# Output projection's first two weight tiles cast inside the planned attention stage, last rows returned by ScalarE, one conditioning vector computed in the recurrent mixer

## The chip, the cores and the metric

The kernel runs on one core of a Trainium2 chip. The core has five engines that work at the same time, each in order through its own queue: TensorE (PE, matrix products into PSUM banks; its weight loads are listed apart as PEld), VectorE (DVE), ScalarE (ACT), GpSimd (POOL) and SyncE (SP, which here only issues DMA transfers). The metric is the device time of one execution in microseconds; lower is better. A few runs are made, and their median is the time given.

## The reference

One sequence of 512 tokens with 1024 channels goes through two layers. Layer 0 mixes tokens by a gated linear recurrence (HGRN2, 8 heads, chunks of 32 tokens); layer 1 by attention in three groups of 8 heads with dilations 1, 4 and 16. Each is followed by a SwiGLU feed-forward block, and each block is modulated by vectors computed from one conditioning vector `c`. Cut to what the change touches:

```python
h = x
for layer in range(DEPTH):                       # 2
    mod = (cond @ ada_w[layer] + ada_b[layer])[:, None, :]
    sh1, sc1, g1, sh2, sc2, g2 = jnp.split(mod, 6, axis=-1)
    u = rms_norm(h, norm_g[layer, 0]) * (1.0 + sc1) + sh1
    y = hgrn2_mixer(...) if layer == 0 else dilated_attention_mixer(u, cos, sin, attn_w_in[0], attn_w_out[0])
    h = h + (1.0 + g1) * rms_norm(y, norm_g[layer, 1])
    u = rms_norm(h, norm_g[layer, 2]) * (1.0 + sc2) + sh2
    h = h + (1.0 + g2) * rms_norm(swiglu_ffn(u, ffn_w_in[layer], ffn_w_out[layer]), norm_g[layer, 3])

def dilated_attention_mixer(u, cos, sin, w_in, w_out):
    # per group: q, k with rope on the first 32 of 128 channels of a head, softmax over a window,
    # then the three groups' outputs weighted by softmax of their log sums
    o = jnp.einsum('gbsh,gbshd->bshd', wts, jnp.stack(outs, axis=0))
    return o.reshape(B, S, D_MODEL) @ w_out
```

All inputs are float32. In what follows, vector (l, v) is the v-th of the six vectors of layer l in the order of the split: (0, 5) is layer 0's last gate `g2`, (1, 4) is layer 1's second scale `sc2`.

## The kernel before

**Products.** A float32 product is made of three products of rounded parts: an operand is split into `hi` (a cast by ScalarE) and `lo` (the rest, a subtraction by VectorE), and `three` (L573) issues hi·hi, hi·lo and lo·hi; hence the three lines L574, L575 and L576 wherever weights are multiplied. `cut` and `split` do the same for activations: `oh` and `ol` are the parts of the attention's output `oT`.

**Weights.** `items` (L505 on) is one list of everything that SyncE loads during the kernel, in order: weight tiles of 1 MB (128 x 2048 numbers), and between them the tiles of `ada_w`, from which the modulation vectors are computed. `weave(ws, others, first, every)` strews the entries of `others` between weight tiles, one for each `every` tiles. Class `Stream` walks the list: a loaded tile occupies one of two `raw` buffers, and the next load is issued when a buffer is released; hi and lo parts occupy one of three places. `process_to` casts a weight tile as a whole (L89, L90), `pieces` in pieces (L109, L110), and runs the work of an `ada` entry where it stands in the list.

**A modulation vector.** A vector (1024 numbers) comes from four `ada` tiles (`ada_item`: two halves of the vector, each from two tiles). A tile gives four multiply-adds of 128 x 512 on VectorE (L390, L392); after two tiles GpSimd sums over the partitions (L394). A scale or shift then becomes a column form by four `to_col` operations per half (L404); a gate is finished by `row_fin` with a 512 KB pair of rows.

**The attention stage** (about 675 to 1105 us) has an order of its own. Class `Plan` takes every operation of the stage as a task with a cost, what it reads and writes, and in some cases a goal time; each task gets a due time from the tasks behind it, and the planner simulates the engines and lays down one order per engine. `next_weights` hands the next raw tile of the list to the plan, `plan.place` a buffer (`"hl"` is one of the three hi/lo places). `sevens` is a unit of one head and one of the groups 1 and 2; it leaves q and k of 128 x 512 in `qk`, of which the first 32 partitions carry the rotary embedding. Those 32 rows are copied to `rows` (an own 128 x 256 tile named `shared`), rotated by VectorE in `turned` (L2015) and brought back: for group 0 by ScalarE, for groups 1 and 2 by DMA on SyncE's queue (L2027), four of 32 KB for a unit.

**The stage's end.** The loop at L2425 runs `condition` up to `heads_end`, the index in `items` behind the last head's tiles; the plan then is laid down (L2428), and the items from `heads_end` on, the four tiles of `attn_w_out`, are taken by `mixer_out` (L684), whose order is written by hand. It multiplies the attention's output with `attn_w_out`: eight slices `kt` of the contraction (one head each), four token blocks in four PSUM banks `y0` for the first 512 columns, then `y1` for the others. Its first tile is taken at kt 0, its second at kt 4, each with a whole cast right there. Between these products the table `tail` puts what is left of the last two heads: `pv_n(6)` and the scores of head 7's group 2 behind kt 0 (L1897, L1812), `merge_r(7)` (L1833 to L1849) behind kt 2, `merge_n(7)` behind kt 3, the transposes `flips_r(7)` (L1861) behind kt 4. ScalarE and VectorE work in the order in which these lines stand.

Of the kernel before, what the change touches and what calls it, by code (L numbers as in the profile page):

```python
# [10 lines left out]
F32 = mybir.dt.float32  # L11
# [12 lines left out]
NH = 8  # L24
# [233 lines left out]
class Place:  # L258
# [8 lines left out]
    @property  # L267
    def t(self):
        return self.box[0]
# [22 lines left out]
def block_kernel(tc, x, c, positions, ada_w, ada_b, norm_g, hgrn_w_in, lower, hgrn_norm_g, hgrn_w_out,  # L292
                 attn_w_in, attn_w_out, ffn_w_in, ffn_w_out, inv_freq, out):
    nc = tc.nc
    act, dve, pool, pe = nc.scalar, nc.vector, nc.gpsimd, nc.tensor
    x2, out2 = x[0], out[0]
    V4 = lambda t: t.rearrange("p (a b) -> p a b", a=4)
    L4 = lambda a: a.rearrange("p (l r) -> p r l", r=4)
    R4 = lambda a: a.rearrange("p (r l) -> p l r", r=4)

    with ExitStack() as ctx:
# [29 lines left out]
        h = base.tile([P, NT, D], F32, name="h")  # L331
# [119 lines left out]
        def ada_seq(*vecs):  # L451

            res, last = [], None
            for l, v in vecs:
                for hf in range(2):
                    res.append([ada_item(l, v, hf, 0)])
                    res.append(([fin_item(*last)] if last else []) + [ada_item(l, v, hf, 1)])
                    last = (l, v, hf)
            return res + [[], [fin_item(*last)]]
# [15 lines left out]
        def weave(ws, others, first, every=1):  # L475

            res, o, n = [], list(others), 0
            for i, w in enumerate(ws):
                res.append(w)
                while i >= first + n * every and o:  # L480
                    res += o.pop(0)
                    n += 1
            return res + [i for g in o for i in g]

        items = []
        W = hgrn_w_in[0]
        hg = []
# [5 lines left out]
        hg_o = [wtok(hgrn_w_out[0], kq, hf * 512) for hf in range(2) for kq in range(2)]  # L493
# [10 lines left out]
            return a, [wrow(ffn_w_out[l], j) for j in range(NF // 2)]  # L504

        gate_loads, gate_fins = ada_halves(0, 5)
        items += weave(hg, ada_seq((0, 2), (0, 4), (0, 3)), 1) + gate_loads[0]
        items += weave(hg_o, gate_loads[1:2], 0)
        f0a, f0b = ffn_ws(0)
        n0 = 2 * PLAIN[0]  # L510
        items += weave(f0a[:n0], gate_loads[2:] + [[fin] for fin in gate_fins], 2) + f0a[n0:]
        items += weave(f0b, ada_seq((1, 1), (1, 0), (1, 4)), 0, 0.69)
        AW = attn_w_in[0]

        def av(g, hf):
# [2 lines left out]
        by_seven = lambda g: g > 0  # L518
# [5 lines left out]
        order, at = [], []  # L524
# [28 lines left out]
        for hd in range(5, NH):  # L553
            pairs(hd)
        woven(late[6:], 2)
        heads_end = len(items)
        items += [wtok(attn_w_out[0], kq, hf * 512) for hf in range(2) for kq in range(2)]
        f1a, f1b = ffn_ws(1)
        items += f1a + weave(f1b[:9], ada_seq((1, 5)), 0) + f1b[9:]
        st = Stream(nc, wp, items, 2, 3)  # L560
# [1078 lines left out]
        for p in range(4):  # L1639
# [11 lines left out]
            for k in range(2):  # L1651
# [5 lines left out]
                if k == 1:  # L1657
                    for i in range(2):
                        n = fl.n + i
                        g = {}  # L1660
# [257 lines left out]
        def ACT(cost, fn, r=(), w=(), **k):  # L1918
            plan.add("ACT", cost, lambda e: fn(), r, w, **k)

        def DVE(cost, fn, r=(), w=(), **k):
            plan.add("DVE", cost, lambda e: fn(), r, w, **k)
# [25 lines left out]
        def done_with_raw():  # L1948
            load_next()
# [40 lines left out]
        def next_weights():  # L1990
            while True:
                item = st.items[at_item[0]]
                at_item[0] += 1
                if item[0] in ("w", "quarters", "half"):
                    return queue.pop(0)
                condition(item)
# [15 lines left out]
        t_of = lambda i: [[a[:, i, k] for a in (th, tl)] for k in range(4)]  # L2012
        t1, T3, T4, t2 = (t_of(i) for i in range(4))

        def turned(g, rows, q, k):  # L2015


            rot = slot("rot", 1, [P, 256], mk)
            DVE(0.37, lambda: dve.stream_shuffle(rot.t, rows.t, [(i + 16) % 32 for i in range(32)]), [rows(i) for i in range(4)], [rot()])
            DVE(0.36, lambda: dve.tensor_mul(rot.t, rot.t, cs[:, 1]), w=[rot()])  # L2020
            DVE(0.36, lambda: dve.tensor_mul(rows.t, rows.t, cs[:, 0]), w=[rows(i) for i in range(4)])
            DVE(0.36, lambda: dve.tensor_add(rows.t, rows.t, rot.t), [rot()], [rows(i) for i in range(4)])
            if g:
                for i, t in enumerate((q, k)):
                    for n in range(2):
                        o = (2 * i + n) * 32
                        COPY(lambda t=t, n=n, o=o: nc.sync.dma_start(t.t[0:32, n * 256:n * 256 + 256], rows.t[o:o + 32]),  # L2027
                             [rows(2 * i + n)], [t(n)])
                return
            for i, t in enumerate((q, k)):  # L2030
                for hf in range(2):
                    def back_to(i=i, t=t, hf=hf):
                        dst, src = t.t[0:32], rows.t[i * 64 + hf * 32:i * 64 + hf * 32 + 32]
                        act.copy(L4(dst)[:, 2 * hf:2 * hf + 2], src.rearrange("p (r l) -> p r l", r=2))
                    ACT(0.62, back_to, [rows(2 * i + hf)], [t(0), t(1)])

        def new_rows():
            def make():
# [5 lines left out]
        def sevens(g, hd):  # L2044
# [53 lines left out]
            def products_2():  # L2098
                first, both, u2, u4 = s_["b"]
                xs = s_["xs"]  # L2100
                rows = new_rows()
                q, k = (slot("qk", 6, [P, S], mk) for _ in range(2))
                heads[hd]["q", g], heads[hd]["k", g] = q, k

                def queries(b, n):
                    sl = (lo, hi)[n]
                    ACT(0.38, lambda: act.activation(rows.t[n * 32:n * 32 + 32], b.t[0:32, lo], AF.Copy, scale=-SCALE), [b()], [rows(n)])
                    ACT(0.36, lambda: act.activation(q.t[:, sl], b.t[:, lo], AF.Copy, scale=-SCALE), [b()], [q(n)])

                def keys(n, src, b):  # L2110
                    sl = (lo, hi)[n]
                    DVE(0.36, lambda: dve.tensor_add(k.t[:, sl], xs.t[:, (lo, hi)[src]], b.t[:, lo]), [xs(src), b()], [k(n)])
                    ACT(0.38, lambda: act.copy(rows.t[64 + n * 32:96 + n * 32], k.t[0:32, sl]), [k(n)], [rows(2 + n)])
                run(first, 1, 3, a_of(1, 0), False)
                queries(first, 0)
                run(u4, 1, 0, t1, False)
                ACT(0.36, lambda: act.copy(xs.t[:, hi], u4.t[:, lo]), [u4()], [xs(1)], urgent=True)
                run(u2, 1, 2, T4, False)
                keys(1, 1, both)
                keys(0, 0, u2)  # L2120
                run(u4, 1, 1, a_of(1, 1), False)
                queries(u4, 1)
                turned(g, rows, q, k)
            return [(prepare_1, products_1), (prepare_2, products_2)]

        def plain(g, hd):
# [275 lines left out]
            ticks.add(n + 11, lambda: [flipped(i, "p0", "PN", range(1, 4), 0), flipped(i, "pn", "PN", range(4), 1)])  # L2402
            ticks.add(n + 12, lambda: sums_n(i))

        steps = []
        for kind, g, i in order:
            if kind == "v":
                steps += [("v", None, None, k, *p) for k, p in enumerate(value_unit(g - 1, i))]
# [4 lines left out]
        for n, (kind, g, hd, k, prepare, go) in enumerate(steps):  # L2413
# [8 lines left out]
            go()  # L2422
            if kind == "qk" and by_seven(g):
                ticks.tick()
        while at_item[0] < heads_end:  # L2425
            condition(st.items[at_item[0]])
            at_item[0] += 1
        with tc.manual_schedule(engines=ORDERED | {mybir.EngineType.SP}):  # L2428
            planned = plan.run()
        st.done, st.taken = heads_end, st.taken + sum(k == "qk" and not by_seven(g) for k, g, _ in order)  # L2430
        for st_ in heads.values():
            for name, p in st_.items():
                if isinstance(p, Place):
# [41 lines left out]
```

## Time and profile before

| | us |
| --- | --- |
| median of three runs | 1515.64 |
| lowest and highest | 1515.46, 1519.24 |
| the profiled execution | 1515.5 |
| its span | 1513.8 |
| TensorE busy in the span | 1480.4 (98%) |
| VectorE, ScalarE, GpSimd busy | 1115.9, 792.1, 197.2 |
| mean granted TensorE clock | 0.994 |

Loads that the change moves, from issue to landing in the median: 1 MB of `ada_w` 5.0 us, 1 MB of `ffn_w_out` 4.8 us. Tables of stretches give the busy microseconds of each engine per 25 us; a timeline gives start and duration of an instruction and, in brackets, how long its engine was idle before it and what ended that. Line numbers are those of the kernel before.

### The profile page before, as it was taken

To read this page: it belongs to the slowest core of one execution; us is meant where nothing else is said; L and a number is where in the kernel's file an instruction comes from. 1 tells how busy PE (TensorE), PEld (TensorE's weight loads), DVE (VectorE), ACT (ScalarE), POOL (GpSimd) and SP (SyncE) were. 2 spreads that over 40 slices of the span, in tenths; PEclk is the share of its full clock that TensorE was granted. 3 is DMA by queue.
4 is the path that set the end of the run, shared out by engine and by line. 5 is a ranking of instruction groups with operands and counts; after the bars stand their busy time and mean duration, and the time that the engine had idled before them with its cause. 6 is when DMAs were issued, how large, how long until landed. Compare 5 with 4: busy or idle time off the path is not lost. (4 is left out here: it accounts for less than half of the span.)

```text
span 1513.8 us, 25130 instructions
## 1 busy us (share of the span) xinstructions
PE 1480.4 (98%) x9807; PEld 1324.4 (87%) x9807; DVE 1115.9 (74%) x1904; ACT 792.1 (52%) x1462; POOL 197.2 (13%) x174
## 2 busy tenths in 40 slices
PE   8999999999999999999999999999979999999998
PEld 6777888898999988778999998999968899999886
DVE  4577767487788787777898888887656968887633
ACT  4433443363555532366648787378745545555231
POOL 1011211031111102140001101010002211110100
PEclk9999999999999999999999999999989999999999
DMA  9654444125333356623254442543323333334531
GB/s 303 181 172 132 160 140 167 56 84 167 112 111 106 115 179 235 236 99 125 88 151 140 133 133 88 164 122 94 92 74 126 92 104 112 111 109 143 198 109 56
DMA packets 210535, 201.35 MB, mean 133 GB/s; under 512 B 8376, under 2 KB 168304, under 8 KB 210160
## 3 DMA queue, kind: packets, MB, share of 16 engines
q1 hardware_dynamic: 207440, 192.97, 40.5%
q10 hardware_dynamic: 1952, 6.65, 1.2%
q8 instruction: 77, 1.26, 0.3%
q0 software_dynamic: 1024, 0.13, 0.2%
q14 instruction: 42, 0.34, 0.1%
HBM read 192.31 MB, written 5.31 MB: 131 GB/s over the span
## 5 line engine op out<-in xcount | busy, mean ns | idle before, releaser
L89 ACT CAST hi<-raw 128x2048 fp32r<-128x2048 f32 x45 | 85.9, 1909 | 144.4 <-DMA raw<-in_ffn_w_out_dram 71.4
L90 DVE TENSOR_TENSOR lo<-raw,hi 128x2048 fp32r<-128x2048 f32 x45 | 107.5, 2392 | 55.4 <-ACT hi L89 55.3
L574 PE MATMUL ps_mm<-uh,hi 128*128 128x512 f32 (+1 forms) x400 | 146.3, 366 | 0.0
L575 PE MATMUL ps_mm<-ul,hi 128*128 128x512 f32 (+1 forms) x400 | 144.3, 361 | 1.0 <-DVE ul L674 1.0
L576 PE MATMUL ps_mm<-uh,lo 128*128 128x512 f32 (+1 forms) x400 | 144.6, 361 | 0.0
L2007 PE MATMUL ps_mm<-apart,hiq 128*128 128x256 f32 (+1 forms) x608 | 142.4, 327 | 0.0
L2007 PEld LDWEIGHTS ps_mm<-apart,hiq 128*128 128x128 f32 x608 | 99.9, 188 | 8.1
L574 PE MATMUL ps_mm<-hi,oh 128*128 128x512 f32 x240 | 95.2, 397 | 6.7 <-ACT hi L89 6.7
L575 PE MATMUL ps_mm<-lo,oh 128*128 128x512 f32 x240 | 95.1, 396 | 3.6 <-DVE lo L90 3.5
L2007 PE MATMUL ps_mm<-apart,loq 128*128 128x256 f32 (+1 forms) x304 | 97.8, 322 | 0.1
L989 PE MATMUL ps_mm<-th,hiq 128*128 128x256 f32 x340 | 93.9, 276 | 0.0
L989 PE MATMUL ps_mm<-tl,hiq 128*128 128x256 f32 x340 | 93.9, 276 | 0.0
L989 PE MATMUL ps_mm<-th,loq 128*128 128x256 f32 x340 | 93.9, 276 | 0.0
L980 DVE TENSOR_TENSOR loq<-raw,hiq 128x1024 fp32r<-128x1024 f32 x68 | 80.2, 1222 | 18.4 <-ACT hiq L976 18.4
L574 PEld LDWEIGHTS ps_mm<-uh,hi 128*128 128x128 f32 x400 | 75.5, 189 | 19.8 <-issue 8.4
L575 PEld LDWEIGHTS ps_mm<-ul,hi 128*128 128x128 f32 x400 | 75.6, 189 | 12.1 <-DVE ul L674 1.4
L576 PEld LDWEIGHTS ps_mm<-uh,lo 128*128 128x128 f32 x400 | 75.5, 189 | 11.4
L960 POOL TENSOR_TENSOR raw<-raw 128x512 f32<-128x512 f32 x34 | 45.0, 1324 | 305.2 <-DVE spare L956 146.5
L976 ACT CAST hiq<-raw 128x1024 fp32r<-128x1024 f32 x68 | 68.0, 1047 | 17.4 <-DVE raw L964 16.5
L2007 PE MATMUL ps_mm<-uh,hiq 128*128 128x256 f32 x256 | 72.5, 283 | 4.0 <-ACT ps_mm L2092 3.0
L2007 PE MATMUL ps_mm<-uh,loq 128*128 128x256 f32 x256 | 71.6, 280 | 0.2 <-DVE loq L2050 0.2
L2007 PE MATMUL ps_mm<-ul,hiq 128*128 128x256 f32 x256 | 71.5, 279 | 0.0
(502 smaller groups left out, 4619.0 us busy)
## 6 DMA issues: line engine op xcount, KB each, us to landing
raw<-in_ada_w_dram SPq DMA_DIRECT2D x40, 1024.0 KB, 5.0
raw<-in_ffn_w_in_dram SPq DMA_DIRECT2D x136, 256.0 KB, 3.4
raw<-in_ffn_w_out_dram SPq DMA_DIRECT2D x22, 1024.0 KB, 4.8
raw<-in_attn_w_in_dram SPq DMA_DIRECT2D x64, 256.0 KB, 4.3
raw<-in_hgrn_w_in_dram SPq DMA_DIRECT2D x12, 1024.0 KB, 5.3
raw<-in_attn_w_in_dram SPq DMA_DIRECT2D x12, 1024.0 KB, 5.0
raw<-in_ffn_w_in_dram SPq DMA_DIRECT2D x10, 1024.0 KB, 5.6
raw<-in_attn_w_in_dram SPq DMA_DIRECT2D x16, 512.0 KB, 5.2
```

Of the source, the lines that this page charges most:

```text
L89: self.nc.scalar.copy(hi, t)
L90: self.nc.vector.tensor_sub(lo, t, hi.bitcast(F32))
L574: pe.matmul(ps, ah, bh, start=start, stop=False, skip_group_check=part)
L575: pe.matmul(ps, ah, bl, start=False, stop=False, skip_group_check=part)
L576: pe.matmul(ps, al, bh, start=False, stop=stop, skip_group_check=part)
L960: pool.tensor_add(r[:, 2], r[:, 2], r[:, 0])
L976: act.copy(hi, src)
L980: dve.tensor_sub(lo, src, hi.bitcast(F32))
L989: pe.matmul(ps, w[x][:, a], us[kt][y], start=begin and kt + m == 0, stop=kt == 3 and m == 2, skip_group_check=True)
L2007: pe.matmul(dst(), x, y, start=begin and i == 0, stop=i == len(todo) - 1, skip_group_check=True)
```

## The change

Three things are edited.

1. **Conditioning.** Vector (1, 4) leaves layer 0's `ffn_w_out` stage (`f0b`) and goes between the four tiles of the recurrent mixer's output projection (`hg_o`), two entries for a tile. Gate (0, 5) stood at the end of the mixer's weights and in `ffn_w_in`'s first tiles; its first two tiles are now in the latter, its last two and its second finish in `f0b`, where `weave` puts an entry for every 0.8 tiles instead of 0.69.
2. **Output projection.** `heads_end` goes. The first two `attn_w_out` tiles are taken by `next_weights` inside the plan and cast there in halves of 128 x 1024 by ScalarE and VectorE, with the plan's end as goal; `mixer_out` finds them in `st.ready`.
3. **Rows.** In the units of groups 1 and 2 of the last head (`hd == NH - 1`) the rotated rows go back by four ScalarE copies of 32 x 256 each, instead of four DMAs.

```diff
         gate_loads, gate_fins = ada_halves(0, 5)
-        items += weave(hg, ada_seq((0, 2), (0, 4), (0, 3)), 1) + gate_loads[0]
-        items += weave(hg_o, gate_loads[1:2], 0)
+        items += weave(hg, ada_seq((0, 2), (0, 4), (0, 3)), 1)
+        items += weave(hg_o, [g for g in ada_seq((1, 4)) if g], 0, 0.5)
         f0a, f0b = ffn_ws(0)
         n0 = 2 * PLAIN[0]
-        items += weave(f0a[:n0], gate_loads[2:] + [[fin] for fin in gate_fins], 2) + f0a[n0:]
-        items += weave(f0b, ada_seq((1, 1), (1, 0), (1, 4)), 0, 0.69)
+        items += weave(f0a[:n0], gate_loads[:2] + [gate_fins[:1]], 2) + f0a[n0:]
+        gate = gate_loads[2:]
+        rest = ada_seq((1, 1), (1, 0))
+        items += weave(f0b, gate + [gate_fins[1:] + rest[0]] + rest[1:], 0, 0.8)
...
-        heads_end = len(items)
         items += [wtok(attn_w_out[0], kq, hf * 512) for hf in range(2) for kq in range(2)]
...
-        def turned(g, rows, q, k):
+        def turned(g, rows, q, k, last=False):
...
-            if g:
+            if g and not last:
                 for i, t in enumerate((q, k)):
                     for n in range(2):
...
                     def back_to(i=i, t=t, hf=hf):
                         dst, src = t.t[0:32], rows.t[i * 64 + hf * 32:i * 64 + hf * 32 + 32]
-                        act.copy(L4(dst)[:, 2 * hf:2 * hf + 2], src.rearrange("p (r l) -> p r l", r=2))
-                    ACT(0.62, back_to, [rows(2 * i + hf)], [t(0), t(1)])
+                        if g:
+                            act.copy(dst[:, hf * 256:hf * 256 + 256], src)
+                        else:
+                            act.copy(L4(dst)[:, 2 * hf:2 * hf + 2], src.rearrange("p (r l) -> p r l", r=2))
+                    ACT(0.38 if g else 0.62, back_to, [rows(2 * i + hf)], [t(hf)] if g else [t(0), t(1)])
...
-                turned(g, rows, q, k)
+                turned(g, rows, q, k, hd == NH - 1)
...
-        while at_item[0] < heads_end:
-            condition(st.items[at_item[0]])
-            at_item[0] += 1
+        for _ in range(2):
+            raw, p = next_weights(), plan.place("hl", 3, lambda: st.part_tiles(0))
+            for n in range(2):
+                two = slice(n * 1024, n * 1024 + 1024)
+                ACT(1.0, lambda raw=raw, p=p, two=two: act.copy(p.t[0][:, two], raw.t[:, two]), [raw()], [p("h", n)], goal=clock[0])
+                DVE(1.15, lambda raw=raw, p=p, two=two: dve.tensor_sub(p.t[1][:, two], raw.t[:, two], p.t[0][:, two].bitcast(F32)),
+                    [raw(), p("h", n)], [p("l", n)], goal=clock[0])
+            done_with_raw()
+            after.append(p)
         with tc.manual_schedule(engines=ORDERED | {mybir.EngineType.SP}):
             planned = plan.run()
-        st.done, st.taken = heads_end, st.taken + sum(k == "qk" and not by_seven(g) for k, g, _ in order)
+        st.ready += [tuple(p.t) for p in after]
+        st.done, st.taken = at_item[0], st.taken + sum(k == "qk" and not by_seven(g) for k, g, _ in order)
```

Since a planner lays down the attention's order, the diff does not show where ScalarE's instructions land. Its rows at the end of the stage before, where `oh` are the parts of the attention's output, `hi` the whole cast of the first `attn_w_out` tile, `ps_a` the banks of transposes, L2107 and L2108 the copies of q out of its product bank into the 32 rows (`shared`) and into `qk`, L2280 the exponentials:

```order
L2113 COPY shared<-qk_10725 32x256 x2
L2280 ACTIVATE h,sN_10528<-h,nN_10183 128x256 x2
L570 CAST oh_11055<-oT_6093 128x512
L570 CAST oh_11056<-oT_6094 128x512
L570 CAST oh_11057<-oT_6095 128x512
L89 CAST hi_11074<-raw_10695 128x2048
L2359 COPY h<-ps_a_10955 128x384
L2107 ACTIVATE shared<-ps_mm_10885 32x256
L2280 ACTIVATE h,sN_10528<-h,nN_10183 128x256
L2280 ACTIVATE h,sN_10528<-h,nN_10183 128x128
L2375 COPY oT_late_6099<-ps_b_10686 128x4x128
L2359 COPY h<-ps_a_10962 128x512
```

The same place now. L2433 are the half casts (`hiq_10842` of the first tile, `hiq_10930` of the second), L2036 the returned rows of group 1:

```order
L2036 COPY qk_10628<-shared 32x256 x2
L2036 COPY qk_10629<-shared 32x256 x2
L2433 CAST hiq_10842<-raw_10695 128x1024
L2433 CAST hiq_10930<-raw_10962 128x1024
L571 CAST oh_11071<-oT_6093 128x512
L571 CAST oh_11072<-oT_6094 128x512
L571 CAST oh_11073<-oT_6095 128x512
L2363 COPY h<-ps_a_10959 128x384
L2433 CAST hiq_10930<-raw_10962 128x1024
L2111 ACTIVATE shared<-ps_mm_10817 32x256
L2117 COPY shared<-qk_10725 32x256 x2
L2111 ACTIVATE shared<-ps_mm_10887 32x256
```

and the rows that follow, where L2112 copies q from its two product banks and L2036 returns the rows of group 2:

```order
L2284 ACTIVATE h,sN_10528<-h,nN_10183 128x256 x3
L2284 ACTIVATE h,sN_10528<-h,nN_10183 128x128
L2379 COPY oT_late_6099<-ps_b_10686 128x4x128
L2112 ACTIVATE qk_10723<-ps_mm_10817 128x256
L2112 ACTIVATE qk_10723<-ps_mm_10887 128x256
L2363 COPY h<-ps_a_10966 128x512
L2036 COPY qk_10723<-shared 32x256 x2
L2036 COPY qk_10725<-shared 32x256 x2
L1824 ACTIVATE h,sR_10429<-h,nR_10383 128x256 x4
```

The whole cast is gone, four half casts stand before and between the `oh` casts, and the copies L2107 and L2108 of q's first bank (`ps_mm_10817`), which stood well before this place, are now L2111 in front of the exponentials and L2112 behind `oT_late`.

SyncE's queue at the same place before (`raw` are the tiles, `qk<-shared` the returned rows):

```order
L69 DMA raw_10695<-in_attn_w_out_dram 128x4x512
L69 DMA raw_10958<-in_attn_w_out_dram 128x4x512
L2027 DMA qk_10628<-shared 32x256 x2
L2027 DMA qk_10629<-shared 32x256 x2
L69 DMA raw_11078<-in_attn_w_out_dram 128x4x512
L2027 DMA qk_10723<-shared 32x256
L2027 DMA qk_10725<-shared 32x256 x2
L2027 DMA qk_10723<-shared 32x256
L69 DMA raw_11215<-in_attn_w_out_dram 128x4x512
```

and now:

```order
L69 DMA raw_10695<-in_attn_w_out_dram 128x4x512
L69 DMA raw_10962<-in_attn_w_out_dram 128x4x512
L69 DMA raw_11030<-in_attn_w_out_dram 128x4x512
L69 DMA raw_11044<-in_attn_w_out_dram 128x4x512
L69 DMA raw_11251<-in_ffn_w_in_dram 128x8x256
```

The tiles' loads stand one behind the other, with none of the eight small DMAs of the last head between them. The whole cast of the second tile, which ScalarE did behind `merge_n(7)`, has no row any more either.

Last, SyncE's queue in the recurrent mixer before:

```order
L69 DMA raw_1918<-in_ada_w_dram 128x4x512
L69 DMA raw_2049<-in_ada_w_dram 128x4x512
L69 DMA raw_2062<-in_hgrn_w_out_dram 128x4x512
L69 DMA raw_2074<-in_ada_w_dram 128x4x512
L69 DMA raw_2080<-in_hgrn_w_out_dram 128x4x512
L69 DMA raw_2204<-in_hgrn_w_out_dram 128x4x512
L69 DMA raw_2210<-in_hgrn_w_out_dram 128x4x512
L69 DMA raw_2387<-in_ffn_w_in_dram 128x8x256
```

and now:

```order
L69 DMA raw_1918<-in_ada_w_dram 128x4x512
L69 DMA raw_2049<-in_hgrn_w_out_dram 128x4x512
L69 DMA raw_2062<-in_ada_w_dram 128x4x512
L69 DMA raw_2074<-in_hgrn_w_out_dram 128x4x512
L69 DMA raw_2197<-in_ada_w_dram 128x4x512
L69 DMA raw_2203<-in_ada_w_dram 128x4x512
L69 DMA raw_2381<-in_hgrn_w_out_dram 128x4x512
L69 DMA raw_2387<-in_ada_w_dram 128x4x512
L69 DMA raw_2393<-in_hgrn_w_out_dram 128x4x512
```

Two more `ada_w` tiles stand ahead of the last tile of `hgrn_w_out`: four of the vector (1, 4) for two of the gate.

2 lines of the change are left out of this document (1 added, 1 removed).

## The prediction

> **What bounds the kernel now.** I read the page first. TensorE is busy for nearly the whole span.
>
> ```profile
> span 1513.8 us, 25130 instructions
> PE 1480.4 (98%) x9807; PEld 1324.4 (87%) x9807; DVE 1115.9 (74%) x1904; ACT 792.1 (52%) x1462; POOL 197.2 (13%) x174
> ```
>
> The edits leave TensorE's products as they are, so they can win at most the 33 us in which it is not busy, and what it loses to a low clock. The second view was the table of 25 us stretches; I read it at the two places that the diff names, the recurrent mixer (225 to 300 us) and the end of the attention (1100 to 1150 us). Behind the stretch come the busy times of PE, PEld, DVE, ACT and POOL, then PE's granted clock.
>
> ```profile
> 225.00:250.00 25.00, 25.00 (x156) 19.64 (x156) 20.03 (x36) 6.19 (x15) 4.70 (x4) 1.00 0.50 170
> 250.00:275.00 25.00, 25.00 (x159) 21.64 (x158) 15.98 (x20) 11.30 (x26) 4.31 (x2) 1.00 0.36 126
> 275.00:300.00 25.00, 25.00 (x114) 20.69 (x113) 9.75 (x15) 9.32 (x26) 2.05 (x3) 1.00 0.13 43
> 1100.00:1125.00 25.00, 17.53 (x79) 13.97 (x79) 15.78 (x54) 10.35 (x25) 2.63 (x4) 0.86 0.23 69
> 1125.00:1150.00 25.00, 24.91 (x125) 21.26 (x126) 9.18 (x13) 9.02 (x16) 0.00 (x0) 0.93 0.55 190
> ```
>
> In the mixer TensorE has no gap at all: nothing is to be won there, only lost. At the attention's end 7.5 us are idle in one stretch, and the clock is down. Third, TensorE's timeline there (start, duration, then in brackets the idle time before it and who ended it):
>
> ```profile
> 1096.69 0.93 PE L2351 MATMUL ps_a<-ident,h 128*128 128x128 f32 x7
> 1100.54 0.51 PE L574 MATMUL ps_mm<-hi,oh 128*128 128x512 f32 x1 [2.92 <-ACT hi L89]
> ...
> 1106.28 0.60 PE L1897 MATMUL ps_b<-h,V 128*128 128x128 f32 x4
> ...
> 1109.59 1.13 PE L1812 MATMUL ps_a<-qk,qk 128*128 128x128 f32 x8 [1.59 <-DMA qk<-shared]
> 1110.47 0.48 PE L574 MATMUL ps_mm<-hi,oh 128*128 128x512 f32 x1
> ...
> 1118.54 0.39 PE L576 MATMUL ps_mm<-hi,oT 128*128 128x512 f32 x1
> 1122.70 0.80 PE L574 MATMUL ps_mm<-hi,oh 128*128 128x512 f32 x1 [3.76 <-ACT hi L89]
> 1125.10 0.80 PE L575 MATMUL ps_mm<-lo,oh 128*128 128x512 f32 x1 [1.60 <-DVE lo L90]
> ...
> 1126.11 0.63 PE L574 MATMUL ps_mm<-hi,oh 128*128 128x512 f32 x1
> ...
> 1128.25 0.50 PE L576 MATMUL ps_mm<-hi,oT 128*128 128x512 f32 x1
> ...
> 1129.28 1.04 PE L1861 MATMUL ps_a<-ident,h 128*128 128x128 f32 x8
> ```
>
> Four waits stand there: 2.92 + 1.59 + 3.76 + 1.60 = 9.87 us. Three are for the parts (hi, lo) of the first two tiles of attn_w_out, one for rows that come back by DMA. They cost more than themselves: the products step by (1118.54 - 1110.47) / 35 = 0.23 us at full speed, but by (1128.25 - 1126.11) / 5 = 0.43 us behind the long wait. The clock column says the same of the whole: 0.14 x 25 + 0.07 x 25 = 5.3 us of full-speed work lost in the two stretches.
>
> **The tail, chained anew.** I compare one interval: from the end of the flips (1096.69 + 0.93 = 1097.62) to the flips of the next merge (L1861, 1129.28), 31.66 us. ScalarE sets it in both kernels, so its rows are the prices:
>
> ```profile
> 1092.68 0.51 ACT L2340 ACTIVATE h<-h,wE 128x256 f32<-128x256 f32 x1 [0.58 <-DVE wE L2327]
> 1093.72 0.37 ACT L2117 COPY xs<-ps_mm 128x256 f32<-128x256 f32 x1 [0.53 <-PE ps_mm L2007]
> ...
> 1095.22 0.82 ACT L2113 COPY shared<-qk 32x256 f32<-32x256 f32 x2
> ...
> 1097.05 1.64 ACT L570 CAST oh<-oT 128x512 fp32r<-128x512 f32 x3
> ...
> 1100.39 0.47 ACT L2359 COPY h<-ps_a 128x384 f32<-128x384 f32 x1
> ...
> 1101.29 0.51 ACT L2280 ACTIVATE h<-h,nN 128x256 f32<-128x256 f32 x1
> ...
> 1102.18 1.06 ACT L2375 COPY oT_late<-ps_b 128x512 f32<-128x512 f32 x1
> 1103.03 0.63 ACT L2359 COPY h<-ps_a 128x512 f32<-128x512 f32 x1
> 1103.56 0.38 ACT L2108 ACTIVATE qk<-ps_mm 128x256 f32<-128x256 f32 x1
> ...
> 1120.76 1.88 ACT L89 CAST hi<-raw 128x2048 fp32r<-128x2048 f32 x1
> ```
>
> A half cast (128x1024) is priced by the same form elsewhere, the tiles' landing by their own view:
>
> ```profile
> L976 ACT CAST hiq<-raw 128x1024 fp32r<-128x1024 f32 x68 | 68.0, 1047 | 17.4 <-DVE raw L964 16.5
> 1070.09 21.59 SPq L69 DMA_DIRECT2D raw<-in_attn_w_out_dram  x2
> DMA to landing us min/median/max: 4.9/5.2/5.6
> ```
>
> Now ScalarE's new order, step by step. The first half cast of tile A (1.05) fits the idle 0.58 + 0.53 of the first two rows, and two copies of ps_mm that stood just before them move behind the casts; so the merges (L2340), which ended as the row at 1095.22 began, end at about 1094.6. Then come four copies of rows of group 1 that were DMAs (4 x 0.41 = 1.64, by L2113's 0.82 x2): 1096.2. Second half of A: 1097.3. First half of B: its load is the second of the SP row, issued by 1070.09 + 21.59 = 1091.7 and landed by 1091.7 + 5.2 = 1096.9, just in time: 1098.3. The first oh is there at 1098.9 and TensorE starts then, 1.6 us earlier than 1100.54. Three oh: 1099.9; copy 128x384: 1100.4; second half of B: 1101.5; rows, two 32x256 copies, rows (0.37 + 0.82 + 0.37): 1103.0; four exponentials (0.89 for two, 1102.18 - 1101.29): 1104.9; oT_late 0.85: 1105.7. Only then come the two copies of ps_mm into qk (0.37 each): 1106.1 and 1106.5; the copy 128x512: 1107.1; and the four copies of rows of group 2: 1108.7.
>
> On TensorE the first two banks of the output and the scores (six products and 0.9 us) last from 1098.9 to about 1101.2. **The third bank is still held by the qk copy that moved**: a new wait from 1101.2 to 1106.1, 4.9 us. Six products (1.4): 1107.5; pv_n (1109.59 - 1.59 - 1106.28 = 1.7, its copy done at 1107.1): 1109.2; the scores of group 2 need the rows of 1108.7 and so start at 1109.2, only 0.4 us before the old 1109.59. After them no tile is waited for: 0.9 + 4 x 12 x 0.23 = 11.9 us to the flips, 1121.1, against 1129.28. The merge does not stop it: its weights were ready 1118.53 - 1109.59 = 8.9 us behind these scores, inside the 11.9. So the tail wins 8.2 us at full clock. It follows that the gain is not in the first half of the interval, where one wait is traded for another, but in the second tile, which used to be cast behind the merge (1120.76).
>
> ```profile
> 1118.53 1.14 DVE L1849 TENSOR_SCALAR h<-h,wE 128x256 f32<-128x256 f32 x4
> ```
>
> The new wait will likely lower the clock once more. Here 2.92 us of idle were followed by slow products, since of the 3.5 us that the stretch from 1100 us lost (0.14 x 25) the spell at its end holds at most (1125 - 1122.7) / 2 = 1.2; 1.59 us were followed by none. The slow spell in the stretch from 1125 us lost 0.07 x 25 = 1.75 us; part of such a spell can fall inside the wait. I take 1.0 off, with bounds 0 and 1.75: **tail -7.2 us** (-8.2 to -6.5). All of it hangs on ScalarE's queue: each microsecond by which B's load lands late delays oh, the qk copies and the rows alike, and so the scores, one for one.
>
> [...]
>
> **Layer 0.** Of the conditioning vector, four 1 MB loads, 16 multiply-adds on VectorE and eight column sums move from layer 0's ffn_w_out stage into the mixer; in exchange two loads with eight multiply-adds leave the mixer for the first ffn_w_in tiles, and two go from there into the ffn_w_out stage. TensorE's waits behind that stage, 545 to 690 us, are the most it can win: 1.9 + 1.2 = 3.1 us.
>
> ```profile
> PE ps_mm L575 <- DVE lo L90: 1.9, 2, 1.3
> PE ps_mm L655 <- DVE xn L649: 1.2, 2, 0.8
> ```
>
> The stage loses two of its twelve ada loads net (four go, two come) and gets a pair of rows of half that size: some 5 to 10 us of transfer less, where two buffers keep the loads back to back. I take 1.2 of the 3.1.
>
> In the mixer VectorE gets eight multiply-adds and eight column sums (with their reads) more:
>
> ```profile
> L392 DVE SCALAR_TENSOR_TENSOR shared<-raw,cond,shared x70: 735/750/755, 237.6 to 1422.1; 128x512 f32<-128x512 f32 x70
> L404 DVE CUSTOM_DVE_ANT_0 diag<-shared,ident x32: 282/286/293, 557.2 to 1022.8; 128x128 f32<-128x128 f32 x32
> ```
>
> 8 x 0.75 + 8 x 0.29 = 8.3 us, into 75 - 20.0 - 16.0 - 9.8 = 29 us of its idle time. SP now has two more 1 MB loads (four for two) ahead of the mixer's last weight tile:
>
> ```profile
> 237.05 0.49 DVE L390 TENSOR_SCALAR shared<-raw,cond 128x512 f32<-128x512 f32 x1 [1.67 <-DMA raw<-in_ada_w_dram]
> 245.31 10.16 SPq L69 DMA_DIRECT2D raw<-in_hgrn_w_out_dram  x3
> 277.88 1.91 ACT L89 CAST hi<-raw 128x2048 fp32r<-128x2048 f32 x1 [1.51 <-PE ps_mm L576]
> 286.31 0.39 PE L574 MATMUL ps_a<-hi,oh 128*128 128x512 f32 x1
> ```
>
> The last issue moves from 255.5 to about 255.5 + 2 x 5.2 = 265.9, landing at 271, and its cast waits for TensorE until 277.88 anyway. The products that use the last two tiles begin at 286.31, four triples (2.7 us) of the other tile first: needed at 289.0, cast by 279.8; with some 2 us for VectorE's half (the lo part, as large as the hi) 7 us of slack cover it. VectorE's queue can still be held by a landing, as in the row at 237.05: 1.67 us there, without a gap of TensorE. So 0 to 1.6 us, one such hold passed on whole; I take 0.4. **Layer 0: -0.8 us** (-3.1 to +1.6).
>
> **Sum.** The profiled execution took 1515.5 us for its span of 1513.8, and the median is 1515.64, the same for this purpose. 1515.5 - 7.2 - 0.8 = **1507.5 us**.
>
> **Rivals.** (1) ScalarE's queue is later than chained: B's load lands 2 to 3 us late, or scheduling on VectorE does it; the scores start after 1111.5 and the tail wins 4 to 5. For it: B's load has a reserve of 0.4 us. Against: none of the four landings took over 5.6. Time 1515.5 - 4.5 - 0.8 = 1510.2. (2) Everything holds: no slow clock and the ffn_w_out waits go: 1515.5 - 8.2 - 3.1 = 1504.2. For it: the waits are behind loads that come earlier. Against: the stage keeps 21 loads and one pair of rows, and the clock fell behind 2.92 us. (3) Slower, in the mixer: two buffers serve weights and conditioning loads alike, and VectorE's adds stand in its queue ahead of the lo casts and the state updates. If all four loads are waited for on VectorE through a whole 5.2 us landing, 21 us of holding meet 29 - 8 = 21 us of idle, and TensorE, which has no gap there, loses what exceeds the 7 us of slack: 14. Time 1515.5 + 14 - 7.2 = 1522. The kernel is slower than before from 7 + 7.2 = 14 us of holding on. Against: the loads are issued ahead, and the one hold of that kind in this stretch took 1.67. (4) The qk copies and the bank wait eat the tail (the clock stays low through kt 1, the merge falls behind): the tail wins 2, time 1513.5, within what can be told from no change.
>
> **How the numbers follow.** What a measurement here can tell from no change is 0.3%, 4.5 us: faster means under 1511.1. Forecast (1505.5 to 1509.5) 0.50; rival 2 0.13; rival 1 0.19, of which 0.17 stays under 1511.1; rival 4 0.12; rival 3 0.06. Faster: 0.50 + 0.13 + 0.17 = 0.80; same: 0.02 + 0.12 = 0.14; slower 0.06. The range reaches from rival 2 with a little more to rival 4's edge: 1503 to 1513; the forecast's own is 1505.5 to 1509.5.
>
> **What would show it.** Right: ScalarE holds four 128x1024 casts between 1091 and 1102; TensorE's waits for hi L89 and lo L90 at the attention's end are gone; a wait of 4 to 6 us before the third output bank, ended by ScalarE's qk copy, with slow products behind; scores of group 2 near 1109 less what layer 0 won; the flips 12 us after them. Wrong: a wait at the scores of group 2 for rows, a wait of kt 4 for merges, TensorE gaps in 225 to 300 us, or ffn_w_out's waits unchanged or larger. The forecast fails first if B's half cast waits for its DMA.

## The result, and where the time went

Over 20 runs each the changed kernel takes 1514.88 us in the median and the kernel before 1515.63; the ratio is 0.9986, with a 95% interval of 0.9975 to 0.9997. A gain of about 0.7 us by the medians, or 2 us by the ratio, stands where 8 were forecast. The profiled execution took 1514.89 us, with a span of 1513.2 us (before 1515.5 and 1513.8).

To see where the expected gain went, I cut both profiled executions at five places where both kernels issue the same TensorE instructions: the transposes of an earlier head in the mixer (the first start of L1621 after 200 us), the turn behind the mixer (first start of L655), the turn behind ffn_w_out (last start of L655), the last flips in the attention (L2351, last start) and the flips of the merge behind them (L1861, first start). In the changed kernel these lines are one to four further down. Times are in us from the start of the span.

| | before | after | stretch before | stretch after | difference |
| --- | --- | --- | --- | --- | --- |
| earlier head's transposes | 223.8 | 223.0 | | | -0.8 |
| turn behind the mixer begins | 302.6 | 309.6 | 78.8 | 86.6 | **+7.8** |
| turn behind ffn_w_out ends | 674.7 | 679.7 | 372.1 | 370.1 | -2.0 |
| last flips in the attention | 1097.3 | 1103.7 | 422.6 | 424.0 | +1.4 |
| flips of the merge | 1129.3 | 1128.4 | 32.0 | 24.7 | **-7.3** |

The end of the attention won 7.3 us, nearly the forecast, and the recurrent mixer lost 7.8, where 0.4 were forecast. So the gain was given back before it was made. First the end of the attention in TensorE's timeline of the changed kernel:

```profile
1103.09 0.93 PE L2355 MATMUL ps_a<-ident,h 128*128 128x128 f32 x7
1104.91 0.50 PE L575 MATMUL ps_mm<-hiq,oh 128*128 128x512 f32 x1 [0.89 <-ACT oh L571]
...
1106.32 1.91 PE L2298 MATMUL ps_a<-qk,qk 128*128 128x128 f32 x8 [0.68 <-ACT h L2363]
...
1108.46 0.63 PE L575 MATMUL ps_mm<-hiq,oh 128*128 128x512 f32 x1
...
1111.92 0.50 PE L575 MATMUL ps_mm<-hiq,oh 128*128 128x512 f32 x1 [1.98 <-ACT qk L2112]
...
1116.42 1.23 PE L1813 MATMUL ps_a<-qk,qk 128*128 128x128 f32 x8
...
1128.41 1.04 PE L1862 MATMUL ps_a<-ident,h 128*128 128x128 f32 x8
```

The waits for hi L89 and lo L90 are gone, and so is the one for rows. In their place stand 0.89 us for the first `oh`, 0.68 us for a bank of scores and the new wait for the third output bank, 1.98 us, ended by the copy of q. Slow products (0.63 us instead of 0.39, at a granted clock of 0.50 from 1108.0 to 1109.9 us) come ahead of that wait.

And the mixer. Below are TensorE's timeline there, then VectorE's, then GpSimd's, all of the changed kernel.

```profile
282.95 0.39 PE L575 MATMUL ps_mm<-hi,oh 128*128 128x512 f32 x1
288.13 1.12 PE L1622 MATMUL ps_a<-ident,aT 128*128 128x128 f32 x4 [4.79 <-DVE aT L1615]
288.89 0.78 PE L576 MATMUL ps_mm<-lo,oh 128*128 128x512 f32 x1
...
292.45 0.63 PE L575 MATMUL ps_a<-hi,oh 128*128 128x512 f32 x1
```

```profile
270.57 0.74 DVE L392 SCALAR_TENSOR_TENSOR shared<-raw,cond,shared 128x512 f32<-128x512 f32 x1
279.15 0.29 DVE L404 CUSTOM_DVE_ANT_0 diag<-shared,ident 128x128 f32<-128x128 f32 x1 [7.83 <-POOL shared L394]
...
280.86 0.17 DVE L589 TENSOR_SCALAR rv<-oss 128x4 f32<-128x4 f32 x1
...
287.38 0.69 DVE L1615 TENSOR_TENSOR aT<-ps_b,orr 128x512 f32<-128x512 f32 x1 [5.45 <-POOL orr L590]
```

```profile
268.26 1.68 POOL L590 TENSOR_TENSOR orr<-rv,expo 128x4 f32<-128x4 f32 x1 [9.17 <-DVE rv L589]
275.87 3.25 POOL L394 PARTITION_ALL_REDUCE shared<-shared  x1 [5.94 <-PE ps_b L1608]
286.30 1.05 POOL L590 TENSOR_TENSOR orr<-rv,expo 128x4 f32<-128x4 f32 x1 [7.18 <-issue]
```

A conditioning vector needs two all-reduces over the partitions (L394) on GpSimd. GpSimd also computes `orr`, the reciprocal root that normalizes a head's output (L590), and without the last head's `orr` VectorE cannot scale that output (L1615) and TensorE cannot transpose it (L1622). The second all-reduce has landed between the last two `orr`. Its data were there at 270.57 + 0.74 = 271.3, but it began only at 275.87, 5.94 us after the `orr` ahead of it had ended; the cause that the view names, a product, is only what came last by semaphores. VectorE stood for 7.83 us at the column sums that follow the all-reduce and came late to `rv`, the operand of the last `orr`. That operand was ready at 280.86 + 0.17 = 281.0, and still `orr` began only at 286.30, 7.18 us behind the all-reduce, with nothing to wait for that the profile shows ("issue"). GpSimd's own queue says the same. Here are, for both lines, the instructions that stand ahead of the operation; EVENT_SEMAPHORE is where the queue has seen the operand (271.3 and 281.0 by VectorE's rows):

```profile
L394 POOLq MODIFY_POOL_CONFIG  x2: 8/8/8, 270.2 to 270.2; - x2
L394 POOLq EVENT_SEMAPHORE  x1: 17/17/17, 271.4 to 271.4; - x1
...
L590 POOLq MODIFY_POOL_CONFIG  x2: 98/98/98, 279.1 to 279.1; - x2
L590 POOLq EVENT_SEMAPHORE  x1: 17/17/17, 281.1 to 281.1; - x1
```

The all-reduce began 4.5 us and `orr` 5.2 us after the queue had passed the semaphore. At each of the two changes between `orr` and the all-reduce stands a pair of short MODIFY_POOL_CONFIG (8 ns each on the way to the all-reduce, 98 ns each on the way back). In the kernel before, the all-reduce ran well ahead of both:

```profile
250.09 3.25 POOL L394 PARTITION_ALL_REDUCE shared<-shared  x1 [13.79 <-DVE shared L392]
267.53 1.06 POOL L589 TENSOR_TENSOR orr<-rv,expo 128x4 f32<-128x4 f32 x1 [14.19 <-DVE rv L588]
276.21 1.01 POOL L589 TENSOR_TENSOR orr<-rv,expo 128x4 f32<-128x4 f32 x1 [7.62 <-DVE rv L588]
```

Behind TensorE's wait of 4.79 us its clock was low as well, as the table of stretches of the changed kernel shows (0.86 from 275 to 300 us, 1.00 in the same stretch before):

```profile
275.00:300.00 25.00, 20.21 (x82) 16.35 (x81) 6.86 (x17) 5.83 (x15) 4.30 (x2) 0.86 0.16 52
...
1100.00:1125.00 25.00, 21.45 (x111) 18.27 (x111) 13.87 (x43) 18.13 (x47) 2.63 (x4) 0.86 0.35 122
1125.00:1150.00 25.00, 25.00 (x134) 21.41 (x133) 13.77 (x33) 9.58 (x18) 0.60 (x1) 1.00 0.48 169
```

The clock lost 0.14 x 25 = 3.5 us there, part of it within the wait, over which it was 0.92. Behind the wait it was 0.50 from 288.13 to 292 us and 0.73 from 292 to 296: 3.87 x 0.50 + 4.00 x 0.27 = 3.0 us, and these with the wait of 4.79 make up the 7.8.

### The profile page after: what moved, and what is told of

It is laid out like the page before. It is cut to its first block, busy times and chain, and to the rows that moved or that the text cites. A ratio compares the mean times of both kernels' runs of the same rounds, so it can differ in the third digit from the quotient of the medians.

```text
span 1513.2 us, 25135 instructions
## 1 busy us (share of the span) xinstructions
PE 1485.4 (98%) x9807; PEld 1329.2 (88%) x9807; DVE 1111.0 (73%) x1906; ACT 795.5 (53%) x1472; POOL 198.8 (13%) x174
## 3 DMA queue, kind: packets, MB, share of 16 engines
q0 software_dynamic: 1024, 0.13, 0.2%
## 5 line engine op out<-in xcount | busy, mean ns | idle before, releaser
L89 ACT CAST hi<-raw 128x2048 fp32r<-128x2048 f32 x43 | 82.1, 1909 | 151.4 <-DMA raw<-in_ffn_w_out_dram 72.5
L90 DVE TENSOR_TENSOR lo<-raw,hi 128x2048 fp32r<-128x2048 f32 x43 | 101.8, 2371 | 62.5 <-ACT hi L89 62.3
L575 PE MATMUL ps_mm<-hi,oh 128*128 128x512 f32 x208 | 82.0, 394 | 1.0 <-ACT hi L89 1.0
L576 PE MATMUL ps_mm<-lo,oh 128*128 128x512 f32 x208 | 82.1, 395 | 0.2 <-DVE lo L90 0.2
```

Of the source, the lines that this page charges most:

```text
L89: self.nc.scalar.copy(hi, t)
L90: self.nc.vector.tensor_sub(lo, t, hi.bitcast(F32))
L575: pe.matmul(ps, ah, bh, start=start, stop=False, skip_group_check=part)
L576: pe.matmul(ps, ah, bl, start=False, stop=False, skip_group_check=part)
```

## The experiments

The theory (S): GpSimd pays about 6 us whenever it goes from an ordinary operation to the all-reduce, and about 7 on the way back (5.94 and 7.18 us in the changed kernel); the move put such a pair on the last head's path. Its rivals: VectorE's added work did it (V), or the loss is spread over mixer and attention and belongs to the tile casts (N).

### The two halves apart

`tail_only` is the changed kernel with the items of the kernel before (the first edit undone):

```diff
-        items += weave(hg, ada_seq((0, 2), (0, 4), (0, 3)), 1)
-        items += weave(hg_o, [g for g in ada_seq((1, 4)) if g], 0, 0.5)
+        items += weave(hg, ada_seq((0, 2), (0, 4), (0, 3)), 1) + gate_loads[0]
+        items += weave(hg_o, gate_loads[1:2], 0)
...
-        items += weave(f0a[:n0], gate_loads[:2] + [gate_fins[:1]], 2) + f0a[n0:]
...
+        items += weave(f0a[:n0], gate_loads[2:] + [[fin] for fin in gate_fins], 2) + f0a[n0:]
+        items += weave(f0b, ada_seq((1, 1), (1, 0), (1, 4)), 0, 0.69)
```

> Conditioning as before (the first edit undone), tile casts and returned rows as changed. Theory S (GpSimd loses time whenever it goes from an ordinary operation to the all-reduce or back, and the mixer's second all-reduce put two such changes on the path of the last head): the mixer has no wait, the tail keeps its gain, 31.66 us from the end of the flips to L1861 becomes about 24.4; ffn_w_out's waits are again 1.9 and 1.2 us: 1515.6 - 7.3 = 1508. Theory V (VectorE's 16 added multiply-adds and 8 column sums are what held the last head): also 1508. Theory N (the loss upstream of the attention's end is spread over attention and mixer and belongs to the tile casts in the plan): a good part of it stays, about 1512.

Measured: 1508.56 us, ratio to the kernel before 0.9941 (0.9920 to 0.9962). The mixer's stretch is back at 78.9 us and the tail's is 24.7, as in the changed kernel. N is out: the tile casts bring their gain and cost nothing upstream that can be told.

`conditioning_only` is the kernel before with the lines of the first edit, nothing else.

> The first edit alone; attention and output projection as before. S and V: TensorE's wait of 4.8 us at the last head's transposes and the slow clock behind it are here, +7 us at the turn behind the mixer, 2 us won back behind ffn_w_out: 1515.6 + 5 = 1520.6. N: the mixer costs little and the time stays near 1515.

Measured: 1521.0 us, ratio 1.0030 (1.0016 to 1.0044), slower. Mixer 85.0 us, the stretch up to the turn behind ffn_w_out 370.6 instead of 372.1, tail 32.2. TensorE's waits between 270 and 300 us, and GpSimd's timeline:

```profile
PE ps_a L1623 <- DVE aT L1616: 4.4, 1, 4.4
```

```profile
268.88 1.68 POOL L591 TENSOR_TENSOR orr<-rv,expo 128x4 f32<-128x4 f32 x1 [9.17 <-DVE rv L590]
276.53 3.25 POOL L394 PARTITION_ALL_REDUCE shared<-shared  x1 [5.96 <-PE ps_b L1609]
286.51 1.05 POOL L591 TENSOR_TENSOR orr<-rv,expo 128x4 f32<-128x4 f32 x1 [6.74 <-issue]
```

The same order and nearly the same gaps, 5.96 and 6.74 us. The sum of the two halves, -0.59% and +0.30%, agrees with the -0.14% of the whole within their intervals.

### Taking the reduction out, and putting one in

`one_reduction_left_out` is the changed kernel without the all-reduce of the second half of vector (1, 4); that half is then not summed over the partitions, and all the rest stays:

```diff
-                if kq == 1:
+                if kq == 1 and (l, v, hf) != (1, 4, 1):
                     pool.partition_all_reduce(a, a, P, bass.bass_isa.ReduceOp.add)
```

> The changed kernel without the all-reduce of the second half of the vector (1, 4); its four loads, 16 multiply-adds and 8 column sums stay, so that half of the vector is not summed over the partitions. S: both head statistics follow each other on GpSimd without a change between them, no wait at the transposes, the turn behind the mixer 7 us earlier: 1514.9 - 7 = 1508, or 1507 with the column sums not waiting. V: the wait at the transposes stays above 3 us and the time near 1514.

Measured: 1507.22 us, ratio 0.9932 (0.9910 to 0.9954). TensorE has no wait in the mixer and its stretch is 78.9 us, with all 16 multiply-adds and all column sums still on VectorE. Its GpSimd:

```profile
268.33 1.68 POOL L590 TENSOR_TENSOR orr<-rv,expo 128x4 f32<-128x4 f32 x1 [9.17 <-DVE rv L589]
277.25 1.01 POOL L590 TENSOR_TENSOR orr<-rv,expo 128x4 f32<-128x4 f32 x1 [7.24 <-DVE rv L589]
```

The last `orr` begins 9 us earlier than the 286.30 of the changed kernel, as soon as VectorE hands it its operand. So the added work on VectorE does not hold the last head by itself.

`extra_reduction` is `tail_only` with one small all-reduce more, in the last head's `core_c`:

```diff
+            if hd == NH - 1:
+                idle = fresh(cp, [P, 4], "oss", 2)
+                pool.tensor_tensor(idle, g["sts"][:, 2, 0:4], expo, op=OP.mult)
+                pool.partition_all_reduce(idle, idle, P, bass.bass_isa.ReduceOp.add)
```

> Tail as changed, conditioning as before, and in the last head one more small all-reduce (128x4, with a 128x4 product ahead of it that makes it late) between the two head statistics; no loads and no VectorE work added. S: all-reduce starts about 6 us behind the product, the last statistic about 7 us behind the all-reduce, TensorE waits 4 to 6 us at the transposes with a slow clock behind: 7 us over the kernel with the tail alone, 1515. V: no wait, within 1 us of the kernel with the tail alone, 1508.

Measured: 1511.43 us, ratio 0.9963 (0.9947 to 0.9979). GpSimd's timeline, and TensorE's waits from 270 to 300 us:

```profile
266.92 1.06 POOL L588 TENSOR_TENSOR orr<-rv,expo 128x4 f32<-128x4 f32 x1 [13.79 <-DVE rv L587]
267.97 0.21 POOL L1609 TENSOR_TENSOR oss<-state,expo 128x4 f32<-128x4 f32 x1
274.39 0.49 POOL L1610 PARTITION_ALL_REDUCE oss<-oss  x1 [6.22 <-issue]
281.80 1.05 POOL L588 TENSOR_TENSOR orr<-rv,expo 128x4 f32<-128x4 f32 x1 [6.92 <-issue]
```

```profile
PE ps_a L1624 <- DVE aT L1617: 2.0, 1, 2.0
```

The two gaps come out as theory S has them, 6.22 and 6.92 us, and here the operand of the all-reduce was on GpSimd itself, so no other engine can be behind the first. The size was missed: TensorE waits 2.0 us where 4 to 6 were expected, and the kernel is about 3 us over `tail_only` instead of 7. The last `orr` begins at 281.80 here and at 286.30 in the changed kernel. GpSimd alone makes this difference of 4.5 us: the all-reduce began 1.5 us earlier, took 0.49 us instead of 3.25, and the gap behind it was 0.3 us shorter. TensorE also came to the transposes earlier, at 281.8 instead of 283.3, so that its wait is shorter by 2.8 us only. Nor was the clock low behind the short wait: it was 1.00 from 275 to 300 us, 0.86 in the changed kernel. That VectorE stood 7.83 us in front of `rv` is not shown to have cost anything: in the changed kernel `rv` was ready 1.9 us behind the all-reduce's end, here 0.6 us, and the gap to `orr` was about the same, 7.18 and 6.92 us. So V is out here too: VectorE has none of the added work, and the wait is there.

### A better place for the reduction

`reduction_later` moves the second half's last tile, all-reduce and column sums behind the mixer:

```diff
-        items += weave(hg_o, [g for g in ada_seq((1, 4)) if g], 0, 0.5)
+        sc14 = [g for g in ada_seq((1, 4)) if g]
+        items += weave(hg_o, sc14[:3], 0, 0.5)
...
-        items += weave(f0a[:n0], gate_loads[:2] + [gate_fins[:1]], 2) + f0a[n0:]
+        items += weave(f0a[:n0], sc14[3:] + gate_loads[:2] + [gate_fins[:1]], 2) + f0a[n0:]
```

> The changed kernel with the second half of the vector (1, 4) (its last ada tile, its all-reduce and its column sums) moved from the mixer's output projection to the third and fourth ffn_w_in tile behind it; the work is the same, no all-reduce stands between the last two head statistics. Theory S: no wait at the transposes, the ffn_w_out stage keeps its 2 us, the tail its 7.3: 1515.6 - 7.3 - 2 = 1506.3, under the kernel with the tail alone (1508.6). Rival: the second all-reduce meets the turn's statistics instead and TensorE waits there, 1510 or more.

Measured: 1506.46 us, ratio 0.9941 (0.9927 to 0.9954). Mixer 78.9 us, the stretch behind it 369.8, tail 25.5. On GpSimd:

```profile
268.35 1.06 POOL L591 TENSOR_TENSOR orr<-rv,expo 128x4 f32<-128x4 f32 x1 [9.76 <-DVE rv L590]
275.60 1.01 POOL L591 TENSOR_TENSOR orr<-rv,expo 128x4 f32<-128x4 f32 x1 [6.19 <-DVE rv L590]
...
341.90 4.11 POOL L394 PARTITION_ALL_REDUCE shared<-shared  x1 [14.65 <-DVE shared L392]
```

The same work as in the changed kernel, with the all-reduce out of the way: this version is faster than both kernels, and its rival is out too: TensorE has no wait between 200 and 300 us and none over 0.6 us up to 400. Against `tail_only` its ratio is the same; the 2 us of the ffn_w_out stage are there in the profile (369.8 against 372.2 us) but the runs do not separate the two.

### What the tail gained by

`rows_by_dma` is `tail_only` with the third edit undone, `rows_only` is the kernel before with the third edit alone:

```diff
-                turned(g, rows, q, k, hd == NH - 1)
+                turned(g, rows, q, k)
```

> Tile casts in the plan, conditioning as before, and the last head's rows by DMA as before, so the third edit alone is undone against the kernel with the tail alone (1508.6). If the third edit carries gain: the scores of group 2 wait for rows again and the time is 1510 or more. If ScalarE's queue is the limit there (eight copies of 0.41 us on it): TensorE starts the output projection up to 1.6 us earlier, waits less for the third bank, but for rows before group 2's scores: 1507.5 to 1509.

> The third edit alone on the kernel before. The wait for rows of 1.6 us at group 2's scores goes, four copies (1.64 us) stand ahead of the oh casts and delay the first products by 1 to 1.6 us: the time stays within 1.5 us of 1515.6. If the returned rows were what the tail gained by: 1512 or less.

Measured: `rows_by_dma` 1509.53 us, ratio 0.9964 (0.9951 to 0.9976), tail 25.0 us; `rows_only` 1515.13 us, ratio 1.000 (0.999 to 1.001), tail 30.8. TensorE's rows with a wait in `rows_by_dma`, and below them those of `rows_only`:

```profile
1098.06 0.50 PE L573 MATMUL ps_mm<-hiq,oh 128*128 128x512 f32 x1 [0.34 <-ACT oh L569]
1099.48 1.16 PE L2296 MATMUL ps_a<-qk,qk 128*128 128x128 f32 x8 [0.69 <-ACT h L2361]
1104.90 0.80 PE L573 MATMUL ps_mm<-hiq,oh 128*128 128x512 f32 x1 [3.33 <-ACT qk L2110]
1110.61 1.13 PE L1811 MATMUL ps_a<-qk,qk 128*128 128x128 f32 x8 [1.13 <-DMA qk<-shared]
```

```profile
1098.52 0.78 PE L574 MATMUL ps_mm<-hi,oh 128*128 128x512 f32 x1 [3.25 <-ACT hi L89]
1118.58 0.51 PE L574 MATMUL ps_mm<-hi,oh 128*128 128x512 f32 x1 [3.76 <-ACT hi L89]
1120.97 0.79 PE L575 MATMUL ps_mm<-lo,oh 128*128 128x512 f32 x1 [1.89 <-DVE lo L90]
```

With the rows by DMA the wait for them is back (1.13 us) and the first products start earlier (0.34 instead of 0.89 us of wait); with the rows alone the waits for both tiles stay. So the gain of the tail is that of the tile casts. The returned rows bring 0.3 us of the tail by one pair of profiles (24.7 against 25.0) and 1.2 by the other (30.8 against 32.0); the runs do not separate either pair.

`early_q` is `reduction_later` with a goal on the last head's copies of q, so that they stand ahead of the `oh` casts:

```diff
-                    ACT(0.38, lambda: act.activation(rows.t[n * 32:n * 32 + 32], b.t[0:32, lo], AF.Copy, scale=-SCALE), [b()], [rows(n)])
-                    ACT(0.36, lambda: act.activation(q.t[:, sl], b.t[:, lo], AF.Copy, scale=-SCALE), [b()], [q(n)])
+                    ACT(0.38, lambda: act.activation(rows.t[n * 32:n * 32 + 32], b.t[0:32, lo], AF.Copy, scale=-SCALE), [b()], [rows(n)], goal=clock[0] if hd == NH - 1 else None)
+                    ACT(0.36, lambda: act.activation(q.t[:, sl], b.t[:, lo], AF.Copy, scale=-SCALE), [b()], [q(n)], goal=clock[0] if hd == NH - 1 else None)
```

> As the kernel with the later reduction, and the last head's two copies of q out of each product bank get the plan's clock as goal, so that they stand ahead of the oh casts. If the wait for the third bank (2.0 us in the changed kernel, 3.5 us where the tail runs with the other conditioning) and the clock behind it set the tail: 1 to 3 us under the kernel with the later reduction, 1504. If ScalarE's queue sets it whatever its order: the wait moves to the scores of group 2 and the time is within 1 us of that kernel, 1506.

Measured: 1506.05 us, ratio 0.9941 (0.9928 to 0.9955), the same as `reduction_later`. TensorE's waits from 1080 to 1140 us:

```profile
PE ps_b L1899 <- ACT h L2364: 1.9, 1, 1.9
PE ps_mm L576 <- DVE qk L2117: 1.0, 1, 1.0
PE ps_mm L578 <- DVE oT L573: 0.6, 1, 0.6
PE ps_mm L576 <- ACT oh L572: 0.4, 1, 0.4
PE ps_mm L576 <- ACT xs L2099: 0.2, 1, 0.2
```

The wait for the copy of q is gone (2.4 us in `reduction_later`), and 1.9 us for the copy in front of `pv_n` and 1.0 us for the next bank came in its place; the waits from 1080 to 1140 us sum to 4.1 us here and to 4.0 there. That fits the second expectation, that ScalarE's queue sets the tail whatever its order, only that the wait moved to `pv_n` and not to the scores. The tail takes 24.1 us instead of 25.5, but three kernels with one and the same tail (the changed one, `tail_only` and `reduction_later`) already lie between 24.7 and 25.5, and the runs show no gain.

## Why the prediction was wrong, step by step

**The tail** was right in size: -7.2 forecast, -7.3 measured, and all of it behind the scores of group 2, as forecast (11.9 us from there to the flips of the merge forecast, 1128.41 - 1116.42 = 12.0 measured). Within its first half the waits differ from the forecast: 2.0 us for the third bank instead of 4.9, because the slow clock (0.50 from 1108.0 to 1109.9 us) and 0.68 us for a bank of scores came ahead of it; the scores of group 2 stood 12.4 us behind the end of the flips where 1109.2 - 1097.6 = 11.6 were forecast. The 1.0 us set aside for a low clock was near the mark: `pv_n`, at a clock of 0.50, took 3.0 us (1113.44 to 1116.42) instead of 1.7 (1.00 in the kernel before), while the third bank came 0.6 us earlier than chained. The merge's slack was read from the start of its last row; from that row's end, 1118.53 + 1.14 = 1119.67, it needs 10.1 us and not 8.9, still inside the 11.9. B's load was in time.

**The ffn_w_out stage** won 2.0 us against 1.2, inside its bounds: of TensorE's waits of 1.9 and 1.2 us there, 1.2 us are left (1.0 for hi, 0.2 for lo).

**The mixer** is the step that failed. It stands there as: "VectorE's queue can still be held by a landing [...] So 0 to 1.6 us, one such hold passed on whole; I take 0.4." Measured were 7.8 us. The step counted the loads on SyncE and the multiply-adds and column sums on VectorE, and its slack of 7 us for the weight tiles held. It did not count the two all-reduces that a vector of four loads brings to GpSimd, of which one is new in the mixer, nor did it look at what else stands in GpSimd's queue there: the last heads' `orr`. `one_reduction_left_out` and `extra_reduction` show that it is this one operation in that one place. The slower rival had the right place, but a wrong mechanism (four landings held on VectorE, 14 us) and a small chance; VectorE was held 7.83 us, by GpSimd and not by a landing, and the last `orr` began 5.3 us after this hold had let its operand through. The prediction's own list of signs had the right one: TensorE gaps in 225 to 300 us.

**The attention** in between was put at nothing; it took 1.4 us more. Over all ten profiles of this study this stretch takes between 421.7 and 424.4 us, and `one_reduction_left_out` (421.9), whose attention is that of the changed kernel (424.0), lies 2.1 us from it; so no edit is shown to explain it, and what remains between the sum of the stages and the medians is not settled.

The sum was 1515.5 - 7.2 - 0.8; with the measured mixer in place of the 0.4 and 2.0 in place of the 1.2 it would have been 1515.5 - 7.2 + 7.8 - 2.0 = 1514.1, within 1 us of the median.

## What to carry to other kernels

When a step is moved, list every engine on which it puts an instruction, the short ones too, and look up what stands on either side in each of these queues. A stretch in which the busiest engine has no gap can only lose: ask there which chain ends last and what its slack is, per engine, before counting added microseconds against idle ones. Where GpSimd has to change between a TENSOR_TENSOR and an all-reduce, put the change where it stands idle longer than the gaps measured here (5.94 to 6.22 us one way, 6.74 to 7.18 the other), and keep an all-reduce away from a short operation that others wait for.

## What was not expected of the hardware

In these runs GpSimd lost time at a change between a TENSOR_TENSOR and the all-reduce, in both directions, and no instruction in the profile of the changed kernel is busy for that long meanwhile: only the pair of MODIFY_POOL_CONFIG, of at most 98 ns each, and an EVENT_SEMAPHORE of 17 ns stand in the queue. In three kernels the gap from the end of the one to the all-reduce was 5.94, 5.96 and 6.22 us though the operand was there 4.5 us or more before the start, and the gap from its end to the next TENSOR_TENSOR 7.18, 6.74 and 6.92 us; without a change between, the last `orr` of the kernel before began 0.15 us behind its operand (276.21 against 275.89 + 0.17).

Where GpSimd had been idle for longer than these gaps, nothing of them shows. In the kernel before, the pair in front of the first all-reduce stood at 236.3, and the all-reduce began at 250.09, after 13.79 us of idle time and 0.24 us behind its operand (249.11 + 0.74). On the way back, the changed kernel's `orr` at 268.26 began after 9.17 us of idle time and 0.16 us behind its operand (267.94 + 0.16). So in these rows the time runs from the change and not from the operand. GpSimd's own issues of DMAs did not count as a change in the kernel before: between its all-reduces at 859.25 and 908.36 stand six of them, no MODIFY_POOL_CONFIG stands there, and the second all-reduce begins 0.03 us behind the last of them:

```profile
907.78 0.55 POOL L2303 DMA_DIRECT2D oR<-scr  x1 [6.10 <-DMA scr<-sN]
908.36 3.18 POOL L1969 PARTITION_ALL_REDUCE shared<-shared  x1
```

What GpSimd does in either gap no run here shows.

TensorE's clock also fell where little idle time was: in the changed kernel's tail 0.89 and 0.68 us of wait are followed by products of 0.63 us (clock 0.50 from 1108.0 to 1109.9 us), while 1.59 us were followed by none in the kernel before (clock 1.00 from 1109.6 to 1111.0). The length of the waits alone does not decide it: `reduction_later` has the same two waits in the same place, and there the eight score products behind them took 1.52 us together, in the changed kernel 1.91. What else decides it was not tried.
